# Weight transfers inside the feed-forwards begun by ScalarE in place of SyncE

## The chip, the cores and the metric

The kernel runs on one core of a Trainium2 chip. A core has five engines that run their own instruction streams side by side: TensorE (PE, matrix products; its weight loads are listed as PEld), VectorE (DVE), ScalarE (ACT), GpSimd (POOL) and SyncE (SP), which here only begins transfers. A transfer is begun by an instruction in the stream of one of these engines and then moved by 16 transfer engines that all streams share. An instruction that waits for a semaphore holds up what stands behind it in the same stream.

The metric is the device time of one execution in microseconds.

## The reference

A trunk of two layers over 256 rows of 1024 float32 values. Each layer is a feed-forward, a mixer (a causal convolution in the first layer, latent attention in the second) and another feed-forward, each with a root-mean-square norm in front:

```python
def swiglu_ffn(h, w1, w3, w2):
    return (jax.nn.silu(h @ w1) * (h @ w3)) @ w2

for i in range(DEPTH):
    h = h + FFN_RES_WEIGHT * swiglu_ffn(rmsnorm(h, ffn_norm1[i]), ffn1_w1[i], ffn1_w3[i], ffn1_w2[i])
    m = rmsnorm(h, mix_norm[i])
    ...
    h = h + FFN_RES_WEIGHT * swiglu_ffn(rmsnorm(h, ffn_norm2[i]), ffn2_w1[i], ffn2_w3[i], ffn2_w2[i])
```

w1 and w3 are 1024 x 2816, w2 is 2816 x 1024, all float32, so the four feed-forwards read about 138 MB of weights.

## The kernel before

**Blocks.** All weights are cut into blocks of 128 x 2048 float32 (1 MB), in a list `blocks` in the order of their use. A block arrives in a `raw` buffer (4 of them, `RAW_BUFS`). TensorE multiplies in a reduced format, so each block is split: ACT casts it to `hi` (L246), DVE subtracts to get the rest, `lo = raw - hi` (L247), each in two pieces of 128 x 1024. `hi` and `lo` have 5 buffers each (`W_BUFS`). Every product is then three matmuls (`mm3`, L332, L335, L336). A raw buffer is free again when the subtraction of its last piece has ended, so the transfer of block n waits for the subtraction of a block some four places earlier.

**Seven-groups.** Some blocks are taken four at a time in a scheme with seven products in place of eight. `load_seven` (L189 to L216) makes seven hi/lo pairs out of four raws, with DVE differences of whole raws in between (L200) and casts at L214; its raws come by `fetched` (L182). One such group stands in the up part of feed-forwards two to four, and one at the start of the down part of all four.

**Gates.** In the up part, silu of one product (ACT, L956) times the other (DVE, L958, in places L258) makes a gate of 128 rows. It has to be turned for the down product: DVE transposes 32 x 32 squares (`gt`, L478), four transfers write it to DRAM (`gd`, L482), one reads it back (`gb` or `rows`, L487), and ACT and DVE split it into `Gh` and `Gl` (L853). The turned residual at the stage ends goes the same way (`hd`, `rows`).

**The order.** A scheduler in the language orders the instructions of each engine from the order in the program, priorities (`urgent`) and extra edges: `order(ins, first)` puts an instruction behind another one in the schedule without a semaphore. All the transfers named so far are SP's, in one stream, and each waits there for its buffer or its source. During the first down part ACT also fills tables for the convolution, in groups of small activations (`diagonals`, L1679 and L1686: `rows<-dpair`).

Of the kernel before, what the change touches and what calls it, by code (L numbers as in the profile page):

```python
# [42 lines left out]
PIECES = 2  # L43
# [46 lines left out]
def trunk(ctx: ExitStack, tc: tile.TileContext, x, xt, first, pos, invf, gfin, wdw,  # L90
          f1w13, f1w2, f2w13, f2w2, cw1, cw2, wa, wuq, wukv, wo, wpair, out):
    nc = tc.nc
# [12 lines left out]
    def uid(s):  # L105
        n_uid[0] += 1
        return f"{s}_{n_uid[0]}"
# [9 lines left out]
    def seven(four):  # L117

        group = {}
        return [("seven", j, four, group) for j in range(7)]  # L120

    blocks = []
    conv_block = {}
    for i in range(2):
        for w13, w2 in ((f1w13, f1w2), (f2w13, f2w2)):

            n_ffn = 2 * i + (w13 is f2w13)
            for cc_ in range(5):
                if cc_ in SEVEN_UP.get(n_ffn, ()):
                    four = [w13[i, m, 2 * cc_ + a_] for a_ in range(2) for m in range(2)]  # L130
                    blocks += seven(four)
                    continue
                for m in range(2):
                    blocks += [w13[i, m, 2 * cc_ + a_] for a_ in range(2)]
            blocks += [w13[i, a_, 10] for a_ in range(2)]
            if n_ffn in SEVEN_DOWN:
                blocks += seven([w2[i, a_] for a_ in range(4)])
            blocks += [w2[i, a_] for a_ in range(4 if n_ffn in SEVEN_DOWN else 0, NF // 2)]
            if w13 is f1w13:
                if i == 0:  # L140

                    for m in (-1, -2, -3, -4, *CONV_TILES):
                        blocks += [cw2[-m - 1] if m < 0 else ("whole", cw1[m])]
                        conv_block[m] = len(blocks) - 1
                else:
                    blocks += [wa[0], wa[1], wa[2][:, :1280], wa[3][:, :1280]]
                    blocks += [wuq[2], wuq[0], wukv[0], wukv[1], wuq[1]]
                    blocks += [wo[a_] for a_ in range(H // 2)]
    loaded = []
# [4 lines left out]
    def order(ins, first):  # L154
        tc.add_manual_dep(ins.ins, first.name, mybir.DependencyInfo(
            mybir.DependencyClass.NoSync, mybir.DependencyReason.DATA), reason="order")

    def behind(ins):

        for first in ahead_of.get(ins.ins.engine, [])[-BEHIND:]:  # L160
            order(ins, first)


    casts = {}

    turns = []
# [14 lines left out]

    def fetched(src):  # L182
        raw = rawp.tile([P, HB], F32, tag="raw", name=uid("raw"))
        dma = nc.sync.dma_start(raw, src)
        if turns:
            order(dma, turns[-1].ins)
        return raw

    def load_seven(j, four, b, pieces):  # L189
        hi = wp.tile([P, HB], F32R, tag="hi", name=uid("hi"))  # L190
        lo = wp.tile([P, HB], F32R, tag="lo", name=uid("lo"))
        n = len(loaded)
        if j == 0:
            b[11], b[12] = fetched(four[0]), fetched(four[1])
        elif j == 1:
            b[22] = fetched(four[3])
        elif j == 2:
            b[21] = fetched(four[2])
        def sub(out, left, right):
            ins = nc.vector.tensor_sub(out, left, right)  # L200
            behind(ins)
            return ins

        if j == 1:
            sub(b[11], b[12], b[11])
            sub(b[12], b[22], b[12])
        elif j == 2:
            sub(b[11], b[22], b[11])
        elif j == 6:
            sub(b[11], b[21], b[11])  # L210
        raw = b[(11, 11, 11, 21, 12, 22, 11)[j]]
        for i in range(pieces):
            c = slice(i * HB // pieces, (i + 1) * HB // pieces)
            casts[n, i] = nc.scalar.copy(hi[:, c], raw[:, c]), sub(lo[:, c], raw[:, c], hi[:, c].bitcast(F32))  # L214
            behind(casts[n, i][0])
        return hi, lo  # L216

    def load(src, pieces=1):
        if isinstance(src, tuple) and src[0] == "seven":
            return load_seven(*src[1:], pieces)  # L220
        if isinstance(src, tuple):
            raw = rawp.tile([P, HB], F32, tag="raw", name=uid("raw"))
            nc.sync.dma_start(raw, src[1])
            return raw
        n = src.shape[-1]
        there = len(loaded) in raws
        raw = raws.pop(len(loaded))[0] if there else rawp.tile([P, HB], F32, tag="raw", name=uid("raw"))
        hi = wp.tile([P, HB], F32R, tag="hi", name=uid("hi"))
        lo = wp.tile([P, HB], F32R, tag="lo", name=uid("lo"))
        if there:  # L230
            pass
        elif len(loaded) < 7:

            for i in range(pieces if len(loaded) < 4 else 1):
                c = slice(i * n // pieces, (i + 1) * n // pieces) if len(loaded) < 4 else slice(n)
                fetch(raw[:, c], src[:, c])
        else:
            dma = nc.sync.dma_start(raw[:, :n], src)
            if turns:

                order(dma, turns[-1].ins)
        for i in range(pieces):
            c = slice(i * n // pieces, (i + 1) * n // pieces)

            low = nc.gpsimd if len(loaded) == conv_block[-4] else nc.vector
            casts[len(loaded), i] = (nc.scalar.copy(hi[:, c], raw[:, c]),  # L246
                                     low.tensor_sub(lo[:, c], raw[:, c], hi[:, c].bitcast(F32)))  # L247
            for cast in casts[len(loaded), i] if len(loaded) not in placed else ():
                behind(cast)
        return hi, lo  # L250
# [17 lines left out]
    def load_to(last):  # L268
        while len(loaded) < last:
            loaded.append(load(blocks[len(loaded)], PIECES))  # L270
# [23 lines left out]
    def fetch(to, src):  # L294

        dma = nc.sync.dma_start(to, src)
        if first_dma:
            order(dma, first_dma[-1].ins)
        first_dma.append(dma)
# [1388 lines left out]
    class Rows512:  # L1688

        n = {"ht": 0, "hb": 0}  # L1690
# [109 lines left out]
def build(shapes):  # L1800
    import concourse.bacc as _bacc

    nc = _bacc.Bacc("TRN2", target_bir_lowering=False, num_devices=1, dynamic_dma_scratch_size=1024)
    args = [nc.dram_tensor(f"in_{n}", s, mybir.dt.from_np(np.dtype(d)), kind="ExternalInput").ap()
            for n, s, d in shapes]
    out = nc.dram_tensor("out", (S, D), F32, kind="ExternalOutput").ap()
    with tile.TileContext(nc, schedule_with_timeline_sim=True) as tc:
        trunk(tc, *args, out)
    return nc
# [9 lines left out]
```

## Time and profile before

| | us |
|---|---|
| median of 3 runs (lowest to highest) | 896.05 (895.89 to 896.4) |
| the profiled execution | 896.07 |
| its span, first to last instruction | 894.3 |
| PE busy | 886.9 |
| DVE busy | 743.1 |
| ACT busy | 571.8 |
| transfer queues, share of 16 engines' span | 61.8% in SP's queue (q1), 0.2% in ACT's (q10) |

The granted clock of TensorE was 0.999 of full speed over the span. Rows of the views shown below name an engine, a line of the program, the operation, what it writes and reads by the program's names without buffer numbers, and how many instructions were put together. A timeline row begins with its start and its length in us, and ends in brackets with the idle time in front of it and what ended that. "SPq" and "ACTq" are the instruction streams of SP and ACT where these begin a transfer or wait.

### The profile page before, as it was taken

To read this page: it belongs to the slowest core of one execution; us is meant where nothing else is said; L and a number is where in the kernel's file an instruction comes from. 1 tells how busy PE (TensorE), PEld (TensorE's weight loads), DVE (VectorE), ACT (ScalarE), POOL (GpSimd) and SP (SyncE) were. 2 spreads that over 40 slices of the span, in tenths; PEclk is the share of its full clock that TensorE was granted. 3 is DMA by queue.
4 is the path that set the end of the run, shared out by engine and by line. 5 is a ranking of instruction groups with operands and counts; after the bars stand their busy time and mean duration, and the time that the engine had idled before them with its cause. 6 is when DMAs were issued, how large, how long until landed. Compare 5 with 4: busy or idle time off the path is not lost.

```text
span 894.3 us, 12241 instructions
## 1 busy us (share of the span) xinstructions
PE 886.9 (99%) x4221; PEld 745.9 (83%) x4221; DVE 743.1 (83%) x1083; ACT 571.8 (64%) x993; POOL 104.2 (12%) x227
## 2 busy tenths in 40 slices
PE   9999999999999999999999999999999999999997
PEld 7888888898988888888888888888899888888886
DVE  6787789579998999999588989995768579989973
ACT  7966458488886646667375566673677566474752
POOL 1000000069962000000010000001400010000000
PEclk9999999999999999999999999999999999999999
DMA  9987629834215864939759369495635349378541
GB/s 330 375 303 274 232 59 355 295 121 172 106 60 194 289 258 144 374 109 388 259 175 339 118 218 357 123 392 182 223 142 189 141 154 342 104 260 317 180 196 48
DMA packets 71055, 198.94 MB, mean 222 GB/s; under 512 B 12369, under 2 KB 41937, under 8 KB 51665
## 3 DMA queue, kind: packets, MB, share of 16 engines
q1 hardware_dynamic: 70560, 197.47, 61.8%
q8 instruction: 33, 0.54, 0.2%
q10 hardware_dynamic: 432, 0.69, 0.2%
q14 instruction: 30, 0.24, 0.1%
HBM read 181.87 MB, written 16.25 MB: 222 GB/s over the span
## 4 chain that ended last, share of the span: by engine, by line
PE 92%; DVE 4%; ACT 2%; DMA 1%; issue 0%; SPq 0%; POOL 0%; DVEq 0%; ACTq 0%
PE u L336 16%; PE u L335 16%; PE u L332 16%; PE o L335 9%; PE o L336 9%; PE o L332 9%; PE gate L1005 2%; PE u L411 2%; DVE acc L1094 2%; PE u L1005 2%; PE tp L446 1%; PE a L335 1%; PE a L332 1%; PE a L336 1%; PE nope L336 1%; PE nope L332 1%
## 5 line engine op out<-in xcount | busy, mean ns | idle before, releaser
L247 DVE TENSOR_TENSOR lo<-raw,hi 128x1024 fp32r<-128x1024 f32 (+1 forms) x236 | 276.2, 1212 | 38.8 <-ACT hi L246 37.6
L246 ACT CAST hi<-raw 128x1024 fp32r<-128x1024 f32 (+1 forms) x238 | 236.8, 1044 | 89.3 <-DMA raw<-in_f2w 30.8
L332 PE MATMUL u<-lo,Xh 128*128 128x512 f32 x612 | 238.4, 389 | 0.1
L336 PE MATMUL u<-hi,Xl 128*128 128x512 f32 x612 | 238.3, 389 | 0.0
L335 PE MATMUL u<-hi,Xh 128*128 128x512 f32 x612 | 238.1, 389 | 0.0
L332 PEld LDWEIGHTS u<-lo,Xh 128*128 128x128 f32 x612 | 114.9, 188 | 24.5 <-ACT Xh L598 0.5
L336 PEld LDWEIGHTS u<-hi,Xl 128*128 128x128 f32 x612 | 114.9, 188 | 24.3 <-DVE Xl L465 0.5
L335 PEld LDWEIGHTS u<-hi,Xh 128*128 128x128 f32 x612 | 114.9, 188 | 23.8
L214 ACT CAST hi<-raw 128x1024 fp32r<-128x1024 f32 x98 | 97.7, 1050 | 51.8 <-DVE raw L200 44.9
L200 DVE TENSOR_TENSOR lo<-raw,hi 128x1024 fp32r<-128x1024 f32 x98 | 115.6, 1216 | 7.1 <-ACT hi L214 7.1
L332 PE MATMUL o<-lo,Gh 128*128 128x512 f32 (+1 forms) x276 | 106.6, 386 | 0.0
L335 PE MATMUL o<-hi,Gh 128*128 128x512 f32 (+1 forms) x276 | 106.5, 386 | 0.0
L336 PE MATMUL o<-hi,Gl 128*128 128x512 f32 (+1 forms) x276 | 106.5, 386 | 0.0
L437 POOL TENSOR_TENSOR ms<-ss 128x1 f32<-128x1 f32 x16 | 8.1, 510 | 597.6 <-ACT junk L429 597.6
L200 DVE TENSOR_TENSOR raw<-raw,raw 128x2048 f32<-128x2048 f32 x28 | 63.9, 2283 | 1.8 <-DMA raw<-in_f2w 0.9
L332 PEld LDWEIGHTS o<-lo,Gh 128*128 128x128 f32 x276 | 51.8, 188 | 10.5
L335 PEld LDWEIGHTS o<-hi,Gh 128*128 128x128 f32 x276 | 51.9, 188 | 10.5
L336 PEld LDWEIGHTS o<-hi,Gl 128*128 128x128 f32 x276 | 51.8, 188 | 10.4
L1094 DVE SCALAR_TENSOR_TENSOR acc<-V,dw,acc 128x128 f32<-128x128 f32 (+1 forms) x174 | 53.9, 391 | 0.0
L1115 ACT ACTIVATE prod<-V,dw 128x128 f32<-128x128 f32 (+1 forms) x128 | 45.6, 415 | 1.8 <-POOL Y L1116 1.0
L956 ACT ACTIVATE s<-u,R 128x512 f32<-128x512 f32 (+1 forms) x48 | 30.9, 647 | 24.8 <-PE u L336 24.1
L797 DVE SCALAR_TENSOR_TENSOR h<-o,rh,h 128x512 f32<-128x512 f32 (+1 forms) x18 | 12.9, 719 | 29.2 <-PE o L336 29.2
(265 smaller groups left out, 1257.7 us busy)
## 6 DMA issues: line engine op xcount, KB each, us to landing
raw<-in_f2w SPq DMA_DIRECT2D x66, 1024.0 KB, 6.2
raw<-in_f1w SPq DMA_DIRECT2D x62, 1024.0 KB, 6.5
raw<-in_cw SPq DMA_DIRECT2D x12, 1024.0 KB, 5.5
gd<-gt SPq DMA_DIRECT2D x160, 64.0 KB, 3.0
gb<-gd SPq DMA_DIRECT2D x24, 256.0 KB, 2.8
rows<-gd SPq DMA_DIRECT2D x16, 256.0 KB, 4.4
raw<-in_wo SPq DMA_DIRECT2D x4, 1024.0 KB, 4.9
hd<-rows SPq DMA_DIRECT2D x56, 64.0 KB, 2.4
```

The costliest lines, as they stand in the source:

```text
L200: ins = nc.vector.tensor_sub(out, left, right)
L214: casts[n, i] = nc.scalar.copy(hi[:, c], raw[:, c]), sub(lo[:, c], raw[:, c], hi[:, c].bitcast(F32))
L246: casts[len(loaded), i] = (nc.scalar.copy(hi[:, c], raw[:, c]), low.tensor_sub(lo[:, c], raw[:, c], hi[:, c].bitcast(F32)))
L247: low.tensor_sub(lo[:, c], raw[:, c], hi[:, c].bitcast(F32)))
L332: mm = nc.tensor.matmul(o, ah, bl, start=start, stop=False, skip_group_check=seeded)
L335: nc.tensor.matmul(o, ah, bh, start=False, stop=False, skip_group_check=seeded)
L336: return nc.tensor.matmul(o, al, bh, start=False, stop=stop, skip_group_check=seeded)
L411: mm = nc.tensor.matmul(o, al if kind == "x" else ah, bl if kind == "l" else bh, start=start and n == 0, stop=stop and n == len(kinds) - 1)
L956: nc.scalar.activation(s[:, :w], u[0, tb][:, :w], AF.Silu, scale=X.r[tb])
L1005: mm = nc.tensor.matmul(u[:, t], w[:, c], X.x[:, k, t], start=(k == 0), stop=(k == KT - 1))
L1094: dve_last.append(nc.vector.scalar_tensor_tensor(out if j == j1 - 1 else y, v, w, y, op0=ALU.mult, op1=ALU.add))
L1115: prods_last.append(nc.scalar.activation(p, v, AF.Copy, scale=w))
```

## The change

Of each feed-forward, the blocks from the ninth to the fourth from its end are entered in a set, `by_act`. Their transfers are begun by ACT (`nc.scalar.dma_start`) in place of SP, and the schedule is told to put each behind the last cast piece of the block three places before. Everything else stays in SP's stream: the first eight and last three blocks of each feed-forward, the convolution's and the attention's weights, the gates and the stage ends. Line numbers behind the new function are larger by 9.

```diff
+    by_act = set()
...
             n_ffn = 2 * i + (w13 is f2w13)
+            begin = len(blocks)
...
             blocks += [w2[i, a_] for a_ in range(4 if n_ffn in SEVEN_DOWN else 0, NF // 2)]
+            by_act.update(range(begin + 8, len(blocks) - 3))
...
     def fetched(src):
         raw = rawp.tile([P, HB], F32, tag="raw", name=uid("raw"))
-        dma = nc.sync.dma_start(raw, src)
-        if turns:
-            order(dma, turns[-1].ins)
+        dma = begin_load(raw, src)
         return raw
+
+    def begin_load(raw, src):
+        n = len(loaded)
+        if n in by_act:
+            dma = nc.scalar.dma_start(raw, src)
+            order(dma, casts[n - 3, PIECES - 1][0].ins)
+        else:
+            dma = nc.sync.dma_start(raw, src)
+            if turns:
+                order(dma, turns[-1].ins)
+        return dma
...
         else:
-            dma = nc.sync.dma_start(raw[:, :n], src)
-            if turns:
-
-                order(dma, turns[-1].ins)
+            begin_load(raw[:, :n], src)
```

88 transfers move: SP's stream shrinks from 302 to 214 rows, ACT's grows from 647 to 737. PE's and POOL's orders are the same as before.

SP before, in the first feed-forward's down group (`gd`, `gb`: a gate's way through DRAM; the raws are the blocks that follow the seven-group):

```order
L482 DMA gd_1136<-gt_1134 32x4x64 x4
L482 DMA gd_1150<-gt_1148 32x4x64 x4
L238 DMA raw_1248<-in_f1w 128x2048
L238 DMA raw_1269<-in_f1w 128x2048
L238 DMA raw_1289<-in_f1w 128x2048
L238 DMA raw_1313<-in_f1w 128x2048
L238 DMA raw_1353<-in_f1w 128x2048
L487 DMA gb_1141<-gd_1136 128x256
```

The first four of these five raws move to ACT; the reading back of the gate (`gb_1141`) then stands behind one raw.

ACT after, at the same place (`hi_1210` and `hi_1229` are casts of the seven-group, `rows_139<-dpair` are the convolution's tables):

```order
L267 COPY p_173_1208<-o_1161 128x512
L226 COPY hi_1210<-raw_1064 128x1024 x2
L1688 ACTIVATE rows_139<-dpair,wpair 128x64 x9
L193 DMA raw_1248<-in_f1w 128x2048
L226 COPY hi_1229<-raw_965 128x1024 x2
L193 DMA raw_1269<-in_f1w 128x2048
L255 COPY hi_1249<-raw_1248 128x1024 x2
L1695 ACTIVATE dpair<-dpair,wpair 128x64
L193 DMA raw_1289<-in_f1w 128x2048
L255 COPY hi_1270<-raw_1269 128x1024
```

Without the three transfers the rows are those of before; the transfer of `raw_1248`, whose casts are `hi_1249`, now has two casts and nine activations ahead of it.

ACT after, at the end of the second feed-forward's up group (`hi_3452` and those before it belong to the group; `s` is a silu, `Gh` a gate's cast); the groups of the third and fourth end in the same way:

```order
L226 COPY hi_3433<-raw_3295 128x1024 x2
L193 DMA raw_3471<-in_f2w 128x2048
L965 ACTIVATE s_3532<-u_3390,R_2792 128x512
L862 COPY Gh_2853<-gb_3386 128x4x128
L226 COPY hi_3452<-raw_3235 128x1024 x2
L255 COPY hi_3472<-raw_3471 128x1024 x2
L193 DMA raw_3492<-in_f2w 128x2048
L193 DMA raw_3512<-in_f2w 128x2048
L193 DMA raw_3560<-in_f2w 128x2048
L255 COPY hi_3493<-raw_3492 128x1024 x2
L965 ACTIVATE s_3546<-u_3391,R_2939 128x512
```

Three transfers stand between the casts of one block and the next; before, they followed each other in SP's stream behind `gb_3386`.

ACT after, ahead of that group (`raw_3237` and `raw_3295` are two of its four raws, `Gh<-rows` is a gate's cast):

```order
L193 DMA raw_3235<-in_f2w 128x2048
L255 COPY hi_3142<-raw_3141 128x1024 x2
L965 ACTIVATE s_3212<-u_3084,R_2939 128x512
L193 DMA raw_3237<-in_f2w 128x2048
L862 COPY Gh_2853<-rows_139 128x4x128
L193 DMA raw_3295<-in_f2w 128x2048
L255 COPY hi_3226<-raw_3225 128x1024 x2
```

A gate's cast and a block's casts now stand behind transfers that wait for a raw buffer, which only SP's stream did before.

## The prediction

> **What bounds the kernel now.** I read the page's busy shares first, then the engines' waits, then stretches of the time line around the places where the weights come latest.
>
> ```profile
> span 894.3 us, 12241 instructions
> PE 886.9 (99%) x4221; PEld 745.9 (83%) x4221; DVE 743.1 (83%) x1083; ACT 571.8 (64%) x993; POOL 104.2 (12%) x227
> ```
>
> TensorE (PE) is busy for 886.9 of 894.3 us; the other 7.4 us are mostly the first transfers and the last output. The waits of PE say the same from the other side:
>
> ```profile
> PE warm L324 <- DVE still L319: 1.0, 1, 1.0
> PE u L411 <- ACT Xh L640: 0.2, 1, 0.2
> ```
>
> These two rows are the whole list (row: engine, line, whom it waited for, us in total, times, longest). Both belong to the first microseconds, before any transfer that the change moves. So whatever gets earlier off PE can give at most 1.2 us, and in truth less; what gets later costs nothing until PE has to wait for a weight. The question is where a raw block may be late, and by how much the change makes it late.
>
> The queues that the change touches:
>
> ```profile
> SPq L238 <- DVE lo L247: 156.7, 56, 15.6
> SPq L482 <- DVE gt L478: 123.6, 38, 14.3
> SPq L482 <- DMA raw<-in_f2w: 11.2, 7, 2.2
> ACT hi L246 <- DMA raw<-in_f2w: 30.8, 27, 4.9
> ACT Gh L853 <- DMA rows<-gd: 16.9, 10, 2.8
> ```
>
> SyncE's queue spends its time waiting: for the subtraction that frees a raw buffer (156.7 us in 56 waits), and for turned gates (123.6 us). ScalarE (ACT) waits 30.8 us for transfers of the second feed-forwards' weights to land, and nobody behind it suffers, since PE does not wait for any of it. A block of the second feed-forwards, from issue to landing (the median of 66, last column):
>
> ```profile
> raw<-in_f2w SPq DMA_DIRECT2D x66, 1024.0 KB, 6.2
> ```
>
> **Part 1, issuing.** 88 transfers of 1 MB leave SP (302 to 214 instructions) and enter ACT's queue. An isolated issue by SP and one by ACT are these:
>
> ```profile
> 353.48 0.33 SPq L238 DMA_DIRECT2D raw<-in_f2w  x1
> 885.98 0.34 ACTq L749 DMA_DIRECT2D out<-rows  x1
> ```
>
> So 88 x 0.33 = 29 us leave SP's queue and 88 x 0.34 = 30 us enter ACT's. If that time lies in ACT's sequencer, beside its casts, it costs nothing; if it holds ACT's datapath too, ACT goes from 571.8 to about 602 of 894 us. Even this is bounded by the fullest place, below; I take 0 with an upper end of 0 there too.
>
> **Part 2, the wait in ACT's queue.** Each moved transfer waits for the subtraction that frees its buffer. On SP such a wait held up only gates; on ACT it holds up every cast, gate and activation written after it. The order of the programs tells what comes after; the time of the released subtraction tells how long. For nearly all of the 88, that subtraction (by its row before) has ended before ACT reaches the transfer. The two places where it has not are in the middle of the second feed-forward, where two seven-group raws now stand ahead of a gate's cast and ahead of the next block's casts:
>
> ```profile
> 310.02 0.69 ACT L956 ACTIVATE s<-u,R 128x512 f32<-128x512 f32 x1
> 310.60 0.61 ACT L853 CAST Gh<-rows 128x512 fp32r<-128x512 f32 x1
> 311.75 2.00 ACT L246 CAST hi<-raw 128x1024 fp32r<-128x1024 f32 x2
> 314.25 2.00 ACT L246 CAST hi<-raw 128x1024 fp32r<-128x1024 f32 x2 [0.50 <-DMA raw<-in_f2w]
> ```
>
> Beside them on DVE, and on PE at the first use of the block cast at 314.25:
>
> ```profile
> 309.20 2.36 DVE L247 TENSOR_TENSOR lo<-raw,hi 128x1024 fp32r<-128x1024 f32 x2 [1.24 <-ACT hi L246]
> 312.84 4.86 DVE L247 TENSOR_TENSOR lo<-raw,hi 128x1024 fp32r<-128x1024 f32 x4 [0.67 <-ACT hi L246]
> ...
> 334.96 0.39 PE L332 MATMUL u<-lo,Xh 128*128 128x512 f32 x1
> ```
>
> The first transfer waits for the subtractions that end at 309.20 + 2.36 = 311.56; the cast of 310.60 behind it comes 1.0 us later (1.3 with the issue). The second waits for the middle of the four from 312.84, at about 315.2; the casts of 314.25 come 1.0 to 1.3 us later. The block cast there is first used by PE at 334.96 (its place counted in program order), 18 us after its first subtraction piece. Cost 0; the cover is four blocks of lead, and without it the cost would be these 1.3 us. In a few more places a silu (0.69, the row of 310.02) or a turned gate trades places with a neighbouring cast or subtraction; the same lead covers them.
>
> **Part 3, places without lead.** The lead is gone at the ends of the seven-groups, where DVE works without a pause and PE follows close behind. Busy shares of two such stretches (columns: stretch, length, then each engine's busy us and instructions):
>
> ```profile
> 133.90:147.00 13.10, 13.10 (x60) 10.84 (x59) 12.36 (x13) 12.48 (x25) 0.00 (x0) 1.00 0.85 318
> 353.00:367.00 14.00, 14.00 (x64) 11.56 (x63) 14.00 (x16) 9.89 (x12) 0.00 (x0) 1.00 0.90 318
> ```
>
> Place A is the first feed-forward's down group. Here ACT is full too (12.48 of 13.10), since nine small activations of the convolution's tables (L1679) stand between casts, and the moved transfer stands behind them:
>
> ```profile
> 134.21 0.35 SPq L238 DMA_DIRECT2D raw<-in_f1w  x1
> raw<-in_f1w SPq DMA_DIRECT2D x1, 1024.0 KB, 4.7
> ```
>
> Then ACT, DVE and PE there:
>
> ```profile
> 134.79 2.01 ACT L214 CAST hi<-raw 128x1024 fp32r<-128x1024 f32 x2
> 136.69 2.27 ACT L1679 ACTIVATE rows<-dpair,wpair 128x64 f32<-128x64 f32 x9
> 138.86 2.00 ACT L214 CAST hi<-raw 128x1024 fp32r<-128x1024 f32 x2
> 140.74 2.02 ACT L246 CAST hi<-raw 128x1024 fp32r<-128x1024 f32 x2
> ...
> 142.87 3.49 DVE L247 TENSOR_TENSOR lo<-raw,hi 128x1024 fp32r<-128x1024 f32 x3
> ...
> 144.94 0.39 PE L332 MATMUL o<-lo,Gh 128*128 128x512 f32 x1
> 145.62 0.39 PE L332 MATMUL o<-lo,Gh 128*128 128x512 f32 x1
> ```
>
> Before, SP issues at 134.21 and the block lands 4.7 later, at 138.91; its casts run from 140.74 and DVE's subtractions from 142.87 (1.16 a piece); PE wants the first piece at 144.94 and the second at 145.62. So the raw may land 140.74 - 138.91 = 1.83 us later before its cast moves, and the cast may begin up to 142.87 - 1.1 = 141.8 before DVE moves: 2.9 us in all. In the new order the transfer stands on ACT behind two casts and the nine activations. What is not in the trace is an ACT transfer with a free buffer behind unfinished ACT work, so I bound it:
> - Early end: the sequencer issues as soon as the waits ahead in its queue are satisfied, whatever the datapath still has to do. The waits ahead (the cast at 134.79 and its raw) are satisfied by 134.8, so the issue is at most 0.6 us later. Cost 0.
> - Late end: it issues when the last of the nine activations has ended, 136.69 + 2.27 = 138.96. It lands at 143.66, casts run 143.76 to 145.76, the first subtraction ends at 143.76 + 1.1 + 1.2 = 146.06, the second at 147.2. PE loses 146.06 - 144.94 = 1.12 us, then (147.2 - 145.62 - 1.12) = 0.46 more. Cost 1.6 us.
>
> I take the early end. The nearest rows are the casts: that of 138.86 ends at 140.86, yet the next starts at 140.74, and the activations end at 138.96 with the next cast started at 138.86. ACT thus takes an instruction in before the one ahead has ended, so its waits are looked at ahead of the datapath; how many places ahead no row says. If issuing holds the datapath, two issues (0.7 us) lie ahead of the casts of 140.74, which the 141.8 above still covers.
>
> [...]
>
> Place B is the end of the three up groups (feed-forwards two to four):
>
> ```profile
> 355.39 2.00 ACT L246 CAST hi<-raw 128x1024 fp32r<-128x1024 f32 x2
> 358.27 2.00 ACT L246 CAST hi<-raw 128x1024 fp32r<-128x1024 f32 x2 [0.88 <-DMA raw<-in_f2w]
> 355.11 2.35 DVE L200 TENSOR_TENSOR lo<-raw,hi 128x1024 fp32r<-128x1024 f32 x2
> 359.71 3.49 DVE L247 TENSOR_TENSOR lo<-raw,hi 128x1024 fp32r<-128x1024 f32 x3
> 363.12 0.70 DVE L478 STREAM_TRANSPOSE gt<-s 128x512 f32<-128x512 f32 x1
> 364.90 0.39 PE L332 MATMUL u<-lo,Xh 128*128 128x512 f32 x1
> ```
>
> Three transfers move behind the casts of 355.39, ahead of those of 358.27. Issued as early as on SP (353.48), nothing changes. The last of the three waits for the subtractions that end at 355.11 + 2.35 = 357.46, 0.8 us before the cast of 358.27 behind it. At the late end the first goes at 355.39 + 2.00 = 357.39, lands at 362.1, and the first piece is subtracted by 364.4, 0.5 us ahead of its use at 364.90: cost 0, or 0.2 in each of three places if it lands half a microsecond slower, as the x66 row's median of 6.2 allows. DVE's turned gate (0.70) moves in between the two pieces of that block; the second piece then ends at 363.9, and PE comes to it at 366.26, six matmuls of 0.227 after 364.90: cost 0.
>
> **Part 4, the gates.** SP, freed of 88 waits, issues gates as soon as they are turned. Less waiting of ACT on them (16.9 us above) is worth nothing, because PE waits for none of it. Two streams now share the transfer engines: a gate's 256 KB in the middle of a 1 MB block delays that block by a quarter of its own moving time, under 1 us of the 4.7; A has 2.9 us to spare, B 0.5 on its path through DVE. Cost 0 to 0.3.
>
> **The sum**: 0 (issuing) + 0 (holds) + 0 (A) + 0 (B) + 0 (gates), against the profiled execution's 896.07 us, which stands 0.02 above the median of the runs. I forecast 896.1 us. Bounds of what is unknown: down to -1.2, up to 1.6 + 0.6 + 0.3 = 2.5, so 898.6.
>
> **The rivals.**
> Rival 1, slower: ACT issues a transfer only when the work ahead of it is done. One mechanism, decided at A, from the point where the issue comes more than 2.9 us after 134.21. It gives 1.6 us at A, up to 0.6 at the three B places: 897.7 to 898.3, say 898.0. For it: ACT's list of rows is strictly in order, and A has no lead. Against it: the overlapping starts of ACT rows.
> Rival 2, faster: gates freed from the wait behind raws, raws freed from the wait behind gates (11.2 us in 7 waits shows that these exist). At most the 1.2 us of PE's waits, all of them before the first moved transfer, so really about 0: 894.9 if all were won.
> [...]
> Rival 3, the change doesn't do what it says: transfers stay where they were in time, since the buffers and not the queue set their start (156.7 us of waiting for subtractions against 11.2 for other transfers). That is my forecast's own time, 896.1; only the gates would tell them apart.
>
> **How the numbers follow.** A difference under 0.2% (1.8 us) is about what a measurement of this kernel can't tell from no change. Forecast with rival 3: 0.64. Rival 1 and delays of its kind in places that I have costed at nothing (a wait held longer than counted, three more down groups like A but without the nine activations): 0.30, nearly all of it above +1.8 us, so slower 0.29. Rival 2: 0.06, with a gain above 1.8 us possible only if PE's own rate changed: faster 0.05. Same takes the rest, 0.66. The range reaches from the bottom of rival 2 (895.0) over rival 1 (898.3) to half a microsecond beyond it for the unlisted delays, 898.8.
>
> **What the profile after would show.** [...] If rival 1 holds, the issue at A stands at 139, the raw lands near 143.7, and PE waits about 1.1 and 0.5 us for subtractions. SP's waits on subtractions fall by well over 100 us and reappear in part before ACT's transfers. ACT's waits for gates shrink. I am wrong if PE waits in a normal chunk, where blocks lead as the one of 334.96 does, or if PE's busy time itself changes.

## The result and the profile after

The changed kernel takes 902.07 us (median of 22 runs, 897.37 to 909.78), the kernel before 896.87 us (22 runs, 895.27 to 900.12). The ratio is 1.0061 with a 95% interval of 1.0049 to 1.0073: 0.5 to 0.7% slower, 5.2 us between the medians, and the runs spread over 12.4 us where those of the kernel before spread over 4.9. The forecast of 896.1 us was wrong, and the time lies above its range.

The profiled execution of the changed kernel is its fastest run, 897.37 us, so its profile shows the mechanism but not the size of the loss. From its page, and the whole list of what PE waits for:

```profile
span 895.6 us, 12202 instructions
PE 887.4 (99%) x4221; PEld 744.9 (83%) x4221; DVE 743.7 (83%) x1083; ACT 571.4 (64%) x993; POOL 104.0 (12%) x227
```

```profile
PE u L341 <- DVE lo L212: 1.1, 2, 0.8
PE warm L333 <- DVE still L328: 1.0, 1, 1.0
```

Busy times are within 0.6 us of those of before. What is new is that PE waits for the subtraction of a seven-group (L212). Some waits of SP and ACT after, then two of the kernel before:

```profile
SPq L491 <- DVE gt L487: 231.7, 36, 16.9
SPq L496 <- DMA gd<-gt: 75.5, 60, 9.2
ACT Gh L862 <- DMA rows<-gd: 29.2, 13, 4.4
ACT Gh L862 <- DMA gb<-gd: 24.0, 12, 4.8
```

```profile
SPq L487 <- DMA gd<-gt: 35.1, 52, 2.0
ACT Gh L853 <- DMA gb<-gd: 14.7, 10, 2.7
```

SP now stands ready for the gates, and waits more for a gate's writes to land: its read-backs wait 75.5 us for them in place of 35.1, 9.2 us at the longest in place of 2.0. Part of that is only that SP, freed of raws, comes to the read-back sooner; how much later the gates land is measured below. ACT waits 29.2 + 24.0 us for gates in place of 16.9 + 14.7. The forecast had these waits shrink.

Where that reaches PE: the end of the up group in the fourth feed-forward. Time lines of ACT, SP, DVE and PE before:

```profile
789.38 0.62 ACT L853 CAST Gh<-gb 128x512 fp32r<-128x512 f32 x1 [1.25 <-DMA gb<-gd]
792.21 2.00 ACT L214 CAST hi<-raw 128x1024 fp32r<-128x1024 f32 x2 [1.32 <-DVE raw L200]
...
786.72 0.34 SPq L487 DMA_DIRECT2D gb<-gd  x1
787.11 9.43 SPq L238 DMA_DIRECT2D raw<-in_f2w  x4
...
793.83 2.35 DVE L200 TENSOR_TENSOR lo<-raw,hi 128x1024 fp32r<-128x1024 f32 x2
...
795.44 0.39 PE L332 MATMUL u<-lo,Xh 128*128 128x512 f32 x1
```

And at the same place after:

```profile
787.16 0.33 ACTq L193 DMA_DIRECT2D raw<-in_f2w  x1
793.05 0.62 ACT L862 CAST Gh<-gb 128x512 fp32r<-128x512 f32 x1 [3.43 <-DMA gb<-gd]
794.15 1.98 ACT L226 CAST hi<-raw 128x1024 fp32r<-128x1024 f32 x2
...
784.54 1.86 SPq L491 DMA_DIRECT2D gd<-gt  x4
789.66 0.34 SPq L496 DMA_DIRECT2D gb<-gd  x1
...
795.22 2.36 DVE L212 TENSOR_TENSOR lo<-raw,hi 128x1024 fp32r<-128x1024 f32 x2 [1.20 <-ACT hi L226]
...
796.50 0.50 PE L341 MATMUL u<-lo,Xh 128*128 128x512 f32 x1 [0.80 <-DVE lo L212]
```

Before, the gate was read back at 786.72 and the next raw went out behind it, at 787.11. After, ACT begins that raw at 787.16 while the gate's writes are still on their way; the read-back goes out at 789.66 and lands at 793.05. The gate's cast `Gh` stands ahead of the group's last casts in ACT's order, as it did before. Then `hi` starts at 794.15 and not 792.21, DVE subtracts from 795.22 and not 793.83, and PE uses the piece at 796.50 and not 795.44, of which 0.80 is a wait. Over the whole group PE loses 1.2 us. The span grew by 1.3.

A second profile of the same program (the first experiment) caught a run of 907.34 us; its list of PE's waits is longer, 8.5 us in sum:

```profile
PE o L341 <- ACT o L267: 2.5, 3, 1.0
PE u L341 <- DVE lo L212: 2.4, 2, 1.2
PE warm L333 <- DVE still L328: 1.0, 1, 1.0
PE u L341 <- DVE s L267: 0.9, 1, 0.9
PE o L341 <- DVE lo L212: 0.7, 3, 0.4
PE o L345 <- DVE rows L373: 0.6, 2, 0.3
PE rb L1160 <- POOL rc L1156: 0.4, 1, 0.4
```

### The profile page after: what moved, and what is told of

Its sections match the earlier page's. It is cut to its first block, busy times and chain, and to the rows that moved or that the text cites. A ratio compares the mean times of both kernels' runs of the same rounds, so it can differ in the third digit from the quotient of the medians.

```text
span 895.6 us, 12202 instructions
## 1 busy us (share of the span) xinstructions
PE 887.4 (99%) x4221; PEld 744.9 (83%) x4221; DVE 743.7 (83%) x1083; ACT 571.4 (64%) x993; POOL 104.0 (12%) x227
## 3 DMA queue, kind: packets, MB, share of 16 engines
q10 hardware_dynamic: 13104, 92.97, 27.6%
## 4 chain that ended last, share of the span: by engine, by line
PE 86%; DVE 6%; DMA 4%; ACT 2%; issue 1%; SPq 1%; ACTq 0%; DVEq 0%
PE u L341 13%; PE u L345 13%; PE u L344 13%; PE o L341 9%; PE o L345 9%; PE o L344 9%; PE u L1014 3%; PE gate L1014 3%; PE u L420 2%; DVE lo L256 2%; DMA gd<-gt 2%; DVE lo L212 1%; PE tp L455 1%; SPq L491 1%; PE pairs L1057 1%
## 5 line engine op out<-in xcount | busy, mean ns | idle before, releaser
L212 DVE TENSOR_TENSOR lo<-raw,hi 128x1024 fp32r<-128x1024 f32 x98 | 115.5, 1214 | 4.6 <-ACT hi L226 4.4
L212 DVE TENSOR_TENSOR raw<-raw,raw 128x2048 f32<-128x2048 f32 x28 | 64.0, 2286 | 0.3
L341 PEld LDWEIGHTS o<-lo,Gh 128*128 128x128 f32 x276 | 51.9, 188 | 10.5
L345 PEld LDWEIGHTS o<-hi,Gl 128*128 128x128 f32 x276 | 51.8, 188 | 10.5
L344 PEld LDWEIGHTS o<-hi,Gh 128*128 128x128 f32 x276 | 51.8, 188 | 10.4
```

The costliest lines, as they stand in the source:

```text
L341: mm = nc.tensor.matmul(o, ah, bl, start=start, stop=False, skip_group_check=seeded)
L344: nc.tensor.matmul(o, ah, bh, start=False, stop=False, skip_group_check=seeded)
L345: return nc.tensor.matmul(o, al, bh, start=False, stop=stop, skip_group_check=seeded)
```

## The experiments

**What was compared.** Theory G: the gates. In two queues a gate's small transfers are slower under raw transfers, the gate's casts and subtractions stand ahead of a seven-group in the fixed orders of ACT and DVE, and PE pays where there is no lead. Theory H: the holds. ACT stands still at the waits of its own transfers. The forecast's rival 1 (issue only after the work ahead) is a third. Each ratio below is against runs of the kernel before in the same session; their medians were 897.48, 896.28, 896.05 and 896.53 us.

Two numbers are worked out for each profile by pairing its records with the rows of the program in order. The first is by how much PE's first use of a block, against the profile of before, gets later across each seven-group (us). The second is the time from the end of a gate's transpose to the landing of its read-back, as a mean over 20 gates: the two of the first feed-forward's fourth chunk, and those of the first, third and fourth chunks in the other three.

```
                            later across the groups, feed-forward           gate trips
profile                    1 down  2 up  2 down  3 up  3 down  4 up  4 down   mean
before                      -      -      -      -      -      -      -       10.2
changed, first profile      0.0    0.7    0.0    0.1    0.0    1.2    0.0     11.3
changed, second profile     2.1    0.0    2.3    0.2    2.5    4.3    0.0     12.1
up groups on SP             0.1    0.0    0.9    0.0    1.0    0.0    1.3     11.4
only up groups on ACT       0.0    0.0    0.0    0.0    0.0    2.4    0.0     10.6
three blocks back           0.0    0.5    1.6    0.0    0.0    0.6    2.9     11.7
up on SP, casts deferred    0.0    0.0    0.0    0.0    0.0    0.0    0.0     11.9
casts deferred              0.0    0.0    1.0    5.4    0.0    1.0    0.0     12.1
raws by GpSimd              0.0    2.5    0.0    7.2    0.0    1.6    0.0     11.1
gates by GpSimd             0.0    0.0    0.0    0.0    0.0    0.8    0.0     13.4
packets of 2 KB             0.0    1.0    0.5    0.0    0.8    1.9    0.0     10.5
packets of 4 KB             0.0    0.0    0.6    0.0    1.0    1.7    0.0     11.2
before, packets of 2 KB     0.0    1.5    0.3    0.0    0.0    0.6    0.6     10.7
```

Nearly all the time is lost in these groups; which ones pay differs from run to run. The mean trip alone does not tell the loss: the kernel with 11.9 loses nothing, that with 10.6 loses 2.4 us. What counts is which gate is late and what stands behind it.

The same pairing shows how much theory H can be worth. Counted are the casts and activations that start within 0.1 us of the end of one of the 88 transfers' issues ahead of them in ACT's order, after ACT stood idle; their idle time is the most that the holds can have cost. The first profile of the changed kernel has three of them, 5.0 us in sum, at 318, 488 and 759 us; the second has five, 6.4 us in sum, at 320, 375, 493, 750 and 767. All come more than 20 us before PE's next loss, and the 2.1 and 2.5 us that the first and the third down group lost in the second profile have no hold in the 80 us ahead of them. The hold at 375, of 0.8 us, delays the silu of a gate that the next down group stands behind; a share of that kind isn't excluded.

**The changed kernel again.** No edit.

> The changed kernel once more, for a second profile of it. Theory G (gates): a gate's way through DRAM (four writes, one read back) now shares the 16 transfer engines with 1 MB blocks that before stood behind it in SyncE's queue; its cast on ACT and its subtraction on DVE come late, and at the ends of the up seven-groups, where DVE has no lead, PE waits. The loss then varies with how the transfers meet: about 902 us, PE waits for lo at L212 in the three up groups, 2 to 8 us in sum, each behind a gate whose trip from transpose to landing is longer than before (8.7 against 6.5 us for the worst one of the first profile). Theory H (holds): ACT's queue stands still at the waits of its own transfers and its casts come late; then the PE waits would stand behind casts that follow such a transfer, with the gates in time.

903.92 us (4 runs, 902.92 to 907.34), ratio 1.0073 (1.0048 to 1.0099). The gate trips grow from 10.2 to 12.1 us in the mean. What was missed: the down groups pay too. ACT at the second feed-forward's down group, second profile of the changed kernel, then before:

```profile
382.74 0.62 ACT L862 CAST Gh<-gb 128x512 fp32r<-128x512 f32 x1 [2.04 <-DMA gb<-gd]
384.61 2.00 ACT L226 CAST hi<-raw 128x1024 fp32r<-128x1024 f32 x2 [1.25 <-DVE raw L212]
```

```profile
378.83 0.62 ACT L853 CAST Gh<-gb 128x512 fp32r<-128x512 f32 x1 [2.74 <-DMA gb<-gd]
380.63 2.00 ACT L214 CAST hi<-raw 128x1024 fp32r<-128x1024 f32 x2 [1.18 <-DVE raw L200]
```

PE is 1.5 us late there by then, but the gate's cast 3.9 and the group's cast behind it 4.0; PE loses 2.3 in the group. The first of the group's own raws is late there too, cast at 378.70 in place of 374.09, but the gate's cast still waited 2.04 us after that.

**Where: the up groups back on SyncE, or alone on ACT.**

```diff
             by_act.update(range(begin + 8, len(blocks) - 3))
+            if n_ffn:
+                by_act.difference_update(range(begin + 8, begin + 20))
```

> The 27 transfers around the three up seven-groups (blocks 9 to 20 of feed-forwards two to four) stay on SyncE, the other 61 on ACT. Theory G, with the up groups as the only place where a late gate reaches PE: 896 to 897 us, as before. If down groups or the first feed-forward carry a part: 898 to 901. Theory H: in between as well, since holds are everywhere.

902.57 us, ratio 1.0056 (1.0039 to 1.0074). That is more than any theory had said. The up groups lose nothing (0.0 in all three), but the down groups carry the loss, so the up groups are not the only place.

```diff
-            by_act.update(range(begin + 8, len(blocks) - 3))
+            if n_ffn:
+                by_act.update(range(begin + 8, begin + 20))
```

> Only those 27 transfers are ACT's. Theory G: nearly the whole loss, 900 to 903 us, PE waits for lo at L212. If the loss lies elsewhere: 896 to 898.

899.83 us, ratio 1.0031 (1.0012 to 1.0050), less than half of the loss and less than theory G had said; in the profile only one up group pays. Each part of the change costs in the groups whose own transfers it moves: 0.9 to 1.3 us in three down groups with the up groups on SyncE, 2.4 in an up group here. A hold theory would allow this too.

**Three blocks back on SyncE.**

```diff
+            if n_ffn:
+                by_act.discard(begin + 19)
```

> As the changed kernel, but the three blocks that follow the seven-groups (one each) are SyncE's again, behind the last gate's read-back. In the first profile these blocks began 0.5 to 2.5 us ahead of that read-back, and the largest PE wait (fourth feed-forward, about 1.1 us) stood behind it. Theory G with these three as the main culprits: 897 to 899 us. If the gates of the chunk before the group, which meet the group's own raws, carry more: 900 to 902.

903.38 us, ratio 1.0068 (1.0049 to 1.0088): above both expectations, nothing won. The overtaking of the last gate by one raw, which the first profile had shown so plainly, is one meeting among many.

**Taking the late gates out of the way.** As the kernel with the up groups on SyncE, and then as the full change, with the order of two gates' casts per feed-forward moved:

```diff
-            for gate in gates[-2 * NT:]:
+            for gate in gates[-3 * NT:]:
                 for ins, cast in zip(gate, casts[n_used[0] + 1, 0]):
                     order(ins, cast.ins)
```

> As the kernel with the up groups' 27 transfers back on SyncE (902.6 us, with PE stalls only in the down groups), and besides, the casts and subtractions of the gates of the seven-group's chunk (two per feed-forward) go behind the second block after the down group, where the gates of the chunk after them already stand. Theory G (late gate, fixed order behind it): no late gate is left ahead of a group, PE waits only at the start, 896 to 898 us. Theory H (ACT's own transfers hold its casts): the holds are unchanged, 901 to 904 us.

896.04 us (10 runs) against 896.28, ratio 1.0000 (0.9988 to 1.0012). 61 transfers are still ACT's and the gates are as late as ever (11.9 us), but they no longer stand ahead of a group, and the whole loss of 5 us is gone. The holds did not stay as they were, though: this profile has none, that of the kernel without the deferral two (2.4 us). So this pair alone leaves up to that much to theory H. The list of PE's waits is one row:

```profile
PE warm L335 <- DVE still L330: 1.0, 1, 1.0
```

> The changed kernel with only those gate casts deferred. Theory G: the stalls in the down groups go, those in the up groups stay: 899 to 901 us, PE waits at L212 behind blocks of the up groups only. Theory H: as the changed kernel, 902 to 904 us.

900.34 us, ratio 1.0042 (1.0018 to 1.0067), as theory G had it: the up groups pay (5.4 and 1.0 in its profile). The profile has a single hold, 1.9 us at 764, long after the group that loses 5.4. What stands ahead of that group is a gate whose trip took 20.4 us (11.7 before). ACT there, before and then with the casts deferred:

```profile
492.02 0.62 ACT L853 CAST Gh<-rows 128x512 fp32r<-128x512 f32 x1 [2.41 <-DMA rows<-gd]
493.05 2.00 ACT L214 CAST hi<-raw 128x1024 fp32r<-128x1024 f32 x2 [0.40 <-PE u L336]
```

```profile
500.20 0.62 ACT L862 CAST Gh<-rows 128x512 fp32r<-128x512 f32 x1 [9.97 <-DMA rows<-gd]
500.73 1.99 ACT L226 CAST hi<-raw 128x1024 fp32r<-128x1024 f32 x2
```

This is theory G without a hold: the cast waits 9.97 us for its gate, and the group's first cast goes right behind it. One down group still loses 1.0, which theory G does not give. There the first of the group's raws was late: ACT issued it at 368.67 (SP before at 366.69), it landed 2.1 us later than before, and its cast began at 376.17 in place of 374.09. So a raw can be the late one as well.

**Whose queue it is.** The 88 transfers begun by GpSimd in ACT's place:

```diff
-            dma = nc.scalar.dma_start(raw, src)
+            dma = nc.gpsimd.dma_start(raw, src)
```

> The same 88 transfers, begun by GpSimd in place of ACT, at the same places of the schedule; nothing on ACT can be held by them. Theory G, where only the two queues matter: gates are as late as in the changed kernel (trips of 8 to 9 us for the last gate of an up group, 15 to 18 for the gates of its own chunk), 900 to 905 us. Theory H: 896 to 898 us.

914.72 us (4 runs), ratio 1.0224 (1.0170 to 1.0277). The order of gate casts against block casts on ACT is nearly that of the changed kernel, nothing of ACT's can be held by its own transfers, and the loss is larger. With the counts above, theory H falls as the main cause. Why the loss is three times as large here is open. The largest part in its profile, 7.2 us in the third feed-forward, stands behind the same gate, whose trip took 18.9 us (11.7 before); its cast waited 9.48 us and began at 501.28.

The kernel before, with the gates' own transfers begun by GpSimd:

```diff
-            dma = nc.sync.dma_start(dv[i], t[32 * i:32 * i + 32, :w].rearrange("p (j c) -> p j c", j=4))
+            dma = (nc.gpsimd if tag == 'g' else nc.sync).dma_start(dv[i], t[32 * i:32 * i + 32, :w].rearrange("p (j c) -> p j c", j=4))
...
-        last_read[0] = nc.sync.dma_start(b[:, :w], d)
+        last_read[0] = (nc.gpsimd if tag == 'g' else nc.sync).dma_start(b[:, :w], d)
```

> The kernel before, with all raws on SyncE as they were and the gates' own transfers (writes and read-back) begun by GpSimd. ACT begins nothing. Theory G: again two queues, gates late under raws, stalls at the group ends, 899 to 905 us, more if GpSimd's issues are slow themselves. Theory H: 896 to 898 us.

896.25 us, ratio 0.9999 (0.9990 to 1.0009): theory G missed, although the gates are the latest of all (13.4 us). The order offers a reason. The schedule came out with the last gate's cast behind three more blocks at each up group (61, 100 and 152 blocks' casts ahead of it, 58, 97 and 149 in the kernel before). ACT at the place of the fourth feed-forward:

```profile
792.60 1.99 ACT L214 CAST hi<-raw 128x1024 fp32r<-128x1024 f32 x2
794.50 1.99 ACT L246 CAST hi<-raw 128x1024 fp32r<-128x1024 f32 x2
797.20 2.00 ACT L246 CAST hi<-raw 128x1024 fp32r<-128x1024 f32 x2 [0.71 <-DMA raw<-in_f2w]
799.10 0.61 ACT L853 CAST Gh<-gb 128x512 fp32r<-128x512 f32 x1
```

The gate's cast stands behind the group's last casts here, and the profile shows 0.8 us lost at this place and nothing elsewhere. So lateness alone costs little; a late gate that stands ahead of a group does.

**All 88 on ACT, all these casts deferred, and its control.** The edit above, and for the up groups:

```diff
                 turn(c, tb, w, s)
+            if c - 1 in seven_up:
+                for gate in gates[-5 * NT:-2 * NT]:
+                    for ins, cast in zip(gate, casts[n_used[0] - 2, 0]):
+                        order(ins, cast.ins)
```

> The changed kernel, all 88 transfers ACT's, with the gates' casts and subtractions taken out of the way of both kinds of groups: in feed-forwards two to four those of the three chunks before the up group go behind the third block after it, and in all four those of the fourth chunk behind the second block after the down group. Theory G: no late gate stands ahead of a group, 895.5 to 897 us, with gates as late as in the changed kernel. Theory H: 901 to 904 us.

905.22 us (4 runs, 904.99 to 905.64).

> The kernel before with the same deferral and all transfers SyncE's. It tells whether the deferral gains by itself: PE waits for nothing there, so all theories say 895.5 to 896.5 us.

905.50 us (4 runs, 904.98 to 905.99). Both missed: deferring so much costs 9 us by itself, 3.2 us in each of the three later down groups, in both kernels alike. But with the gates out of the way the 88 transfers cost nothing (905.22 against 905.50), and the four runs of either kernel lie within 1.1 us of each other, where four of the changed kernel spread over 4.4. In the down groups a loss from the transfers could be hidden under these 3.2 us; the kernel with the up groups on SyncE shows those without that. PE's longest wait with the transfers on ACT, then on SyncE:

```profile
PE o L341 <- DVE lo L212: 4.7, 5, 1.3
```

```profile
PE o L332 <- DVE lo L200: 4.7, 5, 1.3
```

**Why the gates are late: turns by packet.** Packets of each queue in two stretches of the second profile of the changed kernel (q1 is SP's queue, q10 ACT's; columns: packets, MB, share of 16 engines). From 313 to 316 us gate writes and read-backs run beside raws, from 379 to 385 two read-backs one after the other, in 2 KB packets:

```profile
q10 hardware_dynamic: 148, 1.09, 87.0%
q1 hardware_dynamic: 146, 0.17, 15.9%
```

```profile
q10 hardware_dynamic: 283, 2.06, 81.4%
q1 hardware_dynamic: 244, 0.46, 20.3%
```

In these stretches the queues move about as many packets as each other, though 133 of ACT's 148 have 8 KB and SP's 2 KB at most, and so about one seventh and one fifth of the bytes are the gates'. The packets' own records say how long each takes: a raw's 8 KB packet takes 346 ns, a gate's write of 512 bytes 31 and its read-back's 2 KB 105 (means over the run before). Between the first and the last packet of a gate's writes, 512 in number, 46 packets of raws start in the kernel before (mean over the 20 gates), 90 and 113 in the two profiles of the changed kernel. As an estimate, 44 and 67 more packets of 346 ns over 16 engines are 1.0 and 1.4 us; the writes take 3.5 and 4.4 us in place of 2.6, so 1.0 and 1.8 more. The read-back lands 5.4 and 5.6 us after its issue in place of 4.8. The time from the transpose to the last issue of a write hardly changes (2.4 us before, 2.2 and 2.4 after). So in the mean the gates are late in the transfer engines and not in SP's stream.

That the two queues take turns by packet is the author's reading of these counts (148 to 146, 283 to 244); the next runs test it.

Two tries with smaller transfers, in halves (shown) and in quarters (512 in place of 1024):

```diff
-            dma = nc.scalar.dma_start(raw, src)
-            order(dma, casts[n - 3, PIECES - 1][0].ins)
+            for a in range(0, HB, 1024):
+                dma = nc.scalar.dma_start(raw[:, a:a + 1024], src[:, a:a + 1024])
+                order(dma, casts[n - 3, PIECES - 1][0].ins)
```

> The changed kernel with each moved 1 MB transfer begun as two of 128 x 1024, whose packets are 4 KB instead of 8 KB. Theory G in its exact form (two queues with work take turns packet by packet, whatever a packet's size): under a raw stream a gate's packet now waits for 4 KB (160 to 164 ns) instead of 8 KB (346 ns), so its trips under raws shorten and the loss falls to about half, 898 to 900 us. If the two queues share by bytes, or the raws' overtaking alone makes the gates late: no change, 901 to 905 us.

> The same in four transfers of 128 x 512 with packets of 2 KB (about 105 ns), four times the issues on ACT. Turns by packet: loss smaller again, 896 to 899 us. Sharing by bytes: 901 to 905 us. If issues cost ACT something (352 x 0.33 = 116 us in its queue): more than that.

917.3 us and 941.66 us (4 runs each): far outside what either theory of sharing had said, and in the direction of the third case, that issues cost ACT something. They change two things at once, the packets (25776 and 51120 in ACT's queue in place of 13104) and the number of transfers (176 and 352 in place of 88). In quarters the longest landing of a gate's writes after their last issue fell to 5.1 us, from 9.4 and 10.4 in the two profiles of the changed kernel (7.4 before the change), as turns by packet have it. But the holds grow: counted as above, 20 casts and activations start right behind a transfer of ACT's in the halves, with 29.7 us of idle time ahead of them, and 38 with 63.9 us in the quarters, where the changed kernel had three and five with 5.0 and 6.4. The median issue takes 0.43 us in quarters (0.33 in the changed kernel). So with that many transfers the holds of theory H are real. How much of the 21 and 45 us they make was not measured.

So the packet size was changed with one transfer for each block: its column blocks are moved in reverse order. The 92.97 MB of ACT's queue then came in 46896 packets (`a=4`, 2 KB a raw's packet) or 24368 (`a=2`, 4 KB), where the changed kernel has 13104. On SyncE the same views stand in `nc.sync.dma_start`.

```diff
-            dma = nc.scalar.dma_start(raw, src)
+            dma = nc.scalar.dma_start(raw.rearrange("p (a c) -> p a c", a=4)[:, ::-1, :], src.rearrange("p (a c) -> p a c", a=4)[:, ::-1, :])
```

> The changed kernel with the same 88 transfers on ACT, each still one transfer of 1 MB, but with its four column blocks moved in reverse order, so that a packet has 2 KB instead of 8 KB. Turns by packet (a gate's packet waits for one raw packet, of about 105 ns instead of 346): gates in time again, 896 to 898.5 us, PE stalls at the group ends under 2 us in sum. Sharing by bytes, or raws overtaking as such: 902 to 905 us as in the changed kernel.

> The kernel before with the packets of the same 88 transfers at 2 KB, all on SyncE. If small packets cost nothing by themselves: 895.5 to 897.5 us. If they move slower: later than that, and what they cost is to be taken off the kernel with 2 KB packets on ACT.

> The changed kernel with packets of 4 KB (about 162 ns). Turns by packet: between the other two, 897 to 901 us. By bytes: 902 to 905 us.

2 KB on ACT: 900.23 us, ratio 1.0045 (1.0028 to 1.0061). 2 KB on SyncE: 898.96, ratio 1.0030 (1.0015 to 1.0045). 4 KB on ACT: 899.56, ratio 1.0035 (1.0023 to 1.0047). The packets are not all that changes: such an issue takes 0.61 us in place of 0.33, and ACT's holds grow to 15.5 us at most (2 KB). Small packets so moved cost 2.4 us by themselves, more than expected, and 2 KB on ACT misses its expectation by 1.7. Over that control, the move to ACT costs 1.3 us with 2 KB packets, with overlapping intervals, where it costs 5 to 6.5 with 8 KB; and the gate trips are 10.5 us, beside 10.7 for the control and 11.3 to 12.1 for 8 KB. That speaks for turns by packet and against shares by bytes, but no more than that: the 4 KB kernel has trips of 11.2 us and does not lie between the others in time, so the size of the effect is not settled to better than a microsecond or two.

No kernel here is faster than the one before.

## Why the prediction was wrong, point by point

**What bounds it** was right: the time is PE's work and PE's waits. In the first profile PE's busy time stayed (887.4 us). In the second its listed waits grow by 7.3 us and the span by 11.2; the other 3.9 stand in the busy time, 890.8 us for the same 4221 matmuls. The matmul behind the wait at 796.50 in the first profile is recorded longer (0.50 in place of 0.39 us), so waits can stand in the busy time too; that all of the 3.9 us are such is not shown.

**Part 1 (issuing, 0)** holds: ACT's busy time is 571.4 us (571.8 before), and an issue on ACT takes 0.33 us.

**Part 2 (holds, 0, with 1.0 to 1.3 us on two casts)** was overtaken. The gate's cast of 310.60 came at 314.12 in the first profile of the changed kernel, and for another reason than the one predicted:

```profile
314.12 0.62 ACT L862 CAST Gh<-rows 128x512 fp32r<-128x512 f32 x1 [2.87 <-DMA rows<-gd]
314.65 2.00 ACT L255 CAST hi<-raw 128x1024 fp32r<-128x1024 f32 x2
```

It waited 2.87 us for its gate, and the block's cast stood behind it. The lead covered that, as forecast, and PE waits for nothing there. Holds of the kind that it priced came at three other casts, with 5.0 us of idle time at most. That they cost nothing that can be seen is shown by the pair 905.22 and 905.50, within what is said there.

**Part 3, place A (0, early end)** was right, and rival 1 was wrong. ACT's rows there, after:

```profile
133.91 0.34 ACTq L193 DMA_DIRECT2D raw<-in_f1w  x1
134.19 2.00 ACT L226 CAST hi<-raw 128x1024 fp32r<-128x1024 f32 x2
136.10 1.30 ACT L1688 ACTIVATE rows<-dpair,wpair 128x64 f32<-128x64 f32 x5
```

The transfer that stands behind two casts and nine activations in the program went out at 133.91, ahead of all of them. It is 0.3 us earlier than SP's before, and PE lost nothing in this group in this profile (2.1 us in the second, behind gates).

**Part 3, place B (0)**: the raws came in time there too, and still PE waited at B, since the cast that was late was not that of the moved block but of the group ahead of it, behind a late gate (at 353.39, after 2.09 us of waiting for it; 0.62 before). The loss was 0.7 us.

**Part 4, the gates (0 to 0.3)** is the step that failed. It priced only what a gate takes from a raw (a quarter of its moving time), not what raws take from a gate: 44 and 67 more of their packets, of 346 ns each, started between the first and the last packet of its writes. And it dismissed the gates' waits because "PE waits for none of it", though ACT's order, shown ahead of the prediction, has a gate's cast (`Gh_2853`) ahead of the group's casts (`hi_3452`), at a place where the prediction itself says that there is no lead. The term it put at 0 to 0.3 measured 0.7 to 4.3 us at each of two to four groups in a run: the trip of a gate got longer (1.1 and 1.9 us in the mean, up to 6 at single gates), and the group behind its cast waited.

**Rival 2** had the sign of this effect turned round: a gate that is no longer behind raws in one queue is not ahead of them either, and its writes took 3.5 and 4.4 us in place of 2.6. (Its bottom is 894.9 us by its own sum; the range has 895.0.) **Rival 3**'s "only the gates would tell them apart" named the place and not the price. The chance of 0.29 for slower stood for rival 1 and for holds, so it is no credit to the forecast that slower came.

## What to carry to other kernels

Moving bulk transfers to a second issuing engine did not leave the small ones alone here: with both in SP's queue 46 packets of raws started between the first and the last packet of a gate's writes, with the raws in ACT's 90 and 113, and the gate's trip went from 10.2 us to 11.3 and 12.1. Before such a move, list the small transfers whose landing stands, in an engine's order, ahead of work without lead (one gate's cast waited 9.97 us here, and the group's first cast went right behind it), and price their delay there, not in the engine's total waiting time; a few lines of order that put such consumers behind the tight stretch took the whole loss of 5 us away for 61 of the transfers, while deferring more of them cost 9 us in either kernel.

## What was not expected of the hardware

A transfer of ACT's went out while eleven ACT instructions ahead of it had not begun (133.91 against 134.19), so the end of the work ahead did not bound its time there. Eleven is the most in that profile; for 80 of ACT's 91 transfers it is three or fewer.

In the two stretches that were counted, two queues moved about equal numbers of packets and not of bytes (148, of which 133 of 8 KB, to 146 of at most 2 KB; 283 to 244).

The runs of the changed kernel spread over 12.4 us (22 runs; 4.4 in the four of a second session), those with all the casts deferred over 0.7 (4 runs). That the meetings of the two queues make the spread fits the groups that pay from run to run, but was not shown.
